# Gate and up in rows: block products for three of eight pairs of chunks, banks by role, weight buffers in halves

## The chip, the cores and the metric

One core of one Trainium2 chip runs the kernel. The time is device microseconds of one execution; it was measured three times, 2257.39 to 2257.93 us, median 2257.55 us. TensorE (PE) multiplies into eight banks of PSUM, VectorE (DVE) and ScalarE (ACT) work on SBUF and PSUM, GpSimd (POOL) does little here, and SyncE (SP) issues the loads.

## The reference

Two layers over 256 tokens of width 2048, all in float32. Each layer has a normed input projection (retention heads and a linear recurrence), an output projection added to x, and a gated feed-forward part of width 5632, which is 44 blocks of 128:

```
h = _rmsnorm(x, norm2_g[l])
x = x + (silu(h @ ffn_w_gate[l]) * (h @ ffn_w_up[l])) @ ffn_w_down[l]
```

A last norm follows. The change concerns `h @ w_gate` and `h @ w_up`, and how weights are prepared everywhere.

## The kernel before

Every weight matrix is read from memory once, in units of 1 MB (`Unit`): 128 columns of a matrix for all 16 chunks of 128 inputs, laid out as 128 x 2048. A unit is loaded into one of three raw buffers by SP (`load`, L551). `split` then makes two float32r tiles of it: ScalarE copies the upper part (`whi`, L568), VectorE subtracts it from the raw weight (`wlo`, L569), 1024 elements at a time. An activation is split in the same way into a pair (`pair`, L126 to L130). A product is then upper times upper, plus upper times lower, plus lower times upper.

In `column_unit` the weights are the loaded operand and the activations stream: L195 multiplies the upper weight chunk with both parts of the activation (512 columns), L198 the lower weight chunk with the upper activation (256 columns); two and two in turn, four such pairs to a block, 16 chunks to a unit. The result stands in a bank as columns of the layer (128 outputs by 256 tokens, twice) and is joined by `joined_halves` (L178, L179). `v_units` is the exception: there the activations are loaded (128 tokens) and 512 weight columns stream, three matmuls per chunk (L441 to L443), since v is wanted by rows.

The program of each engine is in order. `units` gives the order of the work: per layer v, the input projections, 16 units of the output projection, and then, three times (`THIRDS`), 15, 15 and 14 gate units in turn with as many up units, followed by 16 down units that use those 15 or 14 blocks. Ahead of block 0 and block 2 of a unit the loop issues the two splits of the unit two places later; `split` ends with the load of the unit three places after its own. Work that hangs on a result is put off by a number of blocks (`Ticks.after`). A gate unit ends in a scaling with the inverse root (L504) and a silu (L505); an up unit in two products (L509, L510) and the pair for the down projection.

The first of the output projection's units ends within the second one (`held`), because its last chunk comes late.

## Time and profile before

| | |
|---|---|
| median of three runs | 2257.55 us |
| the profiled execution | 2257.48 us, of it span 2255.7 us |
| PE busy | 2239.1 us, 99% |
| PE's weight loads | 1949.4 us, 86% |
| DVE busy | 1512.5 us, 67% |
| ACT busy | 1127.1 us, 50% |
| DMA | 187 GB/s over the span |
| granted TensorE clock | 0.998 of full speed |

Busy is the sum of an engine's instructions. Matmuls are pipelined, one begins before the one ahead of it is finished, so what a matmul costs is read from start to start in a timeline, not from its length. The same holds, by less, for VectorE and ScalarE.

### The profile page before, as it was taken

To read this page: it belongs to the slowest core of one execution; us is meant where nothing else is said; L and a number is where in the kernel's file an instruction comes from. 1 tells how busy PE (TensorE), PEld (TensorE's weight loads), DVE (VectorE), ACT (ScalarE), POOL (GpSimd) and SP (SyncE) were. 2 spreads that over 40 slices of the span, in tenths; PEclk is the share of its full clock that TensorE was granted. 3 is DMA by queue.
4 is the path that set the end of the run, shared out by engine and by line. 5 is a ranking of instruction groups with operands and counts; after the bars stand their busy time and mean duration, and the time that the engine had idled before them with its cause. 6 is when DMAs were issued, how large, how long until landed. Compare 5 with 4: busy or idle time off the path is not lost.

```text
span 2255.7 us, 31764 instructions
## 1 busy us (share of the span) xinstructions
PE 2239.1 (99%) x12760; PEld 1949.4 (86%) x12760; DVE 1512.5 (67%) x2405; ACT 1127.1 (50%) x1648; POOL 59.8 (3%) x97
## 2 busy tenths in 40 slices
PE   9999999999999999999999999999999999999997
PEld 7888888888888888888888888888888888888886
DVE  6888876666566655666748889766665666556665
ACT  6667544544344443444546665444443444334453
POOL 0010100000000000000000101000000000000000
PEclk9999999999999999999999999999999999999999
DMA  7555555555555555555555554555555555555553
GB/s 286 183 186 181 172 195 191 183 191 189 184 200 187 186 186 189 188 190 179 201 193 179 180 197 165 189 182 192 191 183 195 188 187 184 192 188 190 193 175 112
DMA packets 63140, 422.92 MB, mean 187 GB/s; under 512 B 7312, under 2 KB 7952, under 8 KB 24592
## 3 DMA queue, kind: packets, MB, share of 16 engines
q1 hardware_dynamic: 60912, 414.60, 52.5%
q0 software_dynamic: 1792, 5.24, 0.8%
q8 instruction: 100, 1.64, 0.3%
q10 hardware_dynamic: 288, 1.05, 0.1%
q14 instruction: 48, 0.39, 0.0%
HBM read 418.77 MB, written 2.10 MB: 187 GB/s over the span
## 4 chain that ended last, share of the span: by engine, by line
PE 97%; DVE 1%; issue 0%; DMA 0%; POOL 0%; ACT 0%; SPq 0%; DVEq 0%; POOLq 0%
PE acc_ps L195 62%; PE acc_ps L198 31%; PE v_ps L442 1%; PE v_ps L443 1%; PE v_ps L441 1%; PE sm_ps L331 1%; DVE wlo L569 0%; PE sm_ps L240 0%; DMA raw<-in_w_v_dram 0%; DVE op L130 0%; PE sm_ps L289 0%; PE sm_ps L157 0%; PE sm_ps L241 0%; PE sm_ps L256 0%; PE sm_ps L255 0%
## 5 line engine op out<-in xcount | busy, mean ns | idle before, releaser
L195 PE MATMUL acc_ps<-op,whi 128*128 128x512 f32 x6016 | 1899.8, 397 | 0.0
L198 PEld LDWEIGHTS acc_ps<-op,wlo 128*128 128x128 f32 x6016 | 1129.8, 188 | 263.4
L569 DVE TENSOR_TENSOR wlo<-raw,whi 128x1024 fp32r<-128x1024 f32 (+3 forms) x808 | 950.0, 1187 | 366.6 <-ACT whi L568 362.4
L198 PE MATMUL acc_ps<-op,wlo 128*128 128x256 f32 x6016 | 1188.6, 278 | 0.0
L568 ACT ACTIVATE whi<-raw 128x1024 fp32r<-128x1024 f32 (+3 forms) x808 | 817.3, 1029 | 657.3 <-PE acc_ps L195 578.1
L195 PEld LDWEIGHTS acc_ps<-op,whi 128*128 128x128 f32 x6016 | 920.4, 189 | 4.8 <-DVE op L127 0.7
L406 DVE TENSOR_TENSOR x<-acc_ps,x 128x256 f32<-128x256 f32 x128 | 54.2, 424 | 215.5 <-PE acc_ps L198 215.5
L126 ACT ACTIVATE op<-mix 128x256 fp32r<-128x256 f32 x104 | 43.1, 416 | 167.7 <-DVE mix L510 163.5
L505 ACT ACTIVATE sg<-z 128x256 f32<-128x256 f32 x88 | 36.8, 419 | 161.1 <-DVE z L504 161.1
L179 DVE TENSOR_TENSOR z<-acc_ps,low 128x256 f32<-128x256 f32 x256 | 106.7, 417 | 0.0
L178 ACT ACTIVATE low<-acc_ps 128x256 f32<-128x256 f32 x256 | 93.7, 366 | 0.0
L127 DVE TENSOR_TENSOR op<-mix,op 128x256 fp32r<-128x256 f32 x104 | 44.0, 424 | 42.7 <-ACT op L126 42.6
L509 DVE TENSOR_TENSOR sg<-sg,rs 128x256 f32<-128x256 f32 x88 | 37.4, 425 | 42.6 <-ACT sg L505 42.6
L407 DVE TENSOR_TENSOR x<-acc_ps,x 128x256 f32<-128x256 f32 x128 | 54.2, 424 | 4.3
L150 POOL TENSOR_TENSOR rc<-rc,mhalf 128x2 f32<-128x2 f32 x7 | 5.8, 824 | 1720.7 <-DVE rc L149 1720.7
L442 PE MATMUL v_ps<-wlo,op 128*128 128x512 f32 x128 | 50.1, 391 | 1.1 <-DVE wlo L569 1.1
L441 PE MATMUL v_ps<-whi,op 128*128 128x512 f32 x128 | 50.1, 396 | 0.5 <-ACT op L129 0.4
L443 PE MATMUL v_ps<-whi,op 128*128 128x512 f32 x128 | 50.1, 391 | 0.0
L510 DVE TENSOR_TENSOR mix<-z,sg 128x256 f32<-128x256 f32 x88 | 36.7, 417 | 0.0
L504 DVE TENSOR_TENSOR z<-z,rs 128x256 f32<-128x256 f32 x88 | 36.7, 417 | 0.0
L129 ACT ACTIVATE op<-x,par 128x256 fp32r<-128x256 f32 x64 | 31.2, 496 | 2.6 <-DMA par<-in_par_dram 1.8
L173 DVE TENSOR_TENSOR acc<-acc,sq 128x256 f32<-128x256 f32 x73 | 30.6, 420 | 1.6 <-ACT sq L172 1.0
(116 smaller groups left out, 698.9 us busy)
## 6 DMA issues: line engine op xcount, KB each, us to landing
raw<-in_w_gate_dram SPq DMA_DIRECT2D x88, 1024.0 KB, 4.8
raw<-in_w_up_dram SPq DMA_DIRECT2D x88, 1024.0 KB, 4.8
raw<-in_w_in_dram SPq DMA_DIRECT2D x80, 1024.0 KB, 4.8
raw<-in_w_down_dram SPq DMA_DIRECT2D x64, 960.0 KB, 4.7
raw<-in_w_out_dram SPq DMA_DIRECT2D x32, 1024.0 KB, 4.8
raw<-in_w_down_dram SPq DMA_DIRECT2D x32, 896.0 KB, 4.6
raw<-in_w_v_dram SPq DMA_DIRECT2D x12, 1024.0 KB, 4.8
raw<-in_w_v_dram SPq DMA_DIRECT2D x16, 256.0 KB, 6.0
```

Source lines behind the costliest of these rows:

```text
L127: V.tensor_tensor(out=t[:, 1, :], in0=x_ap, in1=t[:, 0, :].bitcast(F32), op=ALU.subtract)
L178: S.activation(out=low, in_=ps[:, T : 2 * T], func=AF.Copy)
L179: V.tensor_tensor(out=z, in0=ps[:, 0:T], in1=low, op=ALU.add)
L195: PE.matmul(u.ps, lhsT=u.hi[:, k * P : (k + 1) * P], rhs=operand(k).rearrange("p a t -> p (a t)"), start=k == order[0], stop=False)
L198: PE.matmul(u.ps[:, T : 2 * T], lhsT=u.lo[:, k * P : (k + 1) * P], rhs=operand(k)[:, 0, :], start=False, stop=k == order[-1])
L406: V.tensor_tensor(out=X[:, k, :], in0=ps[:, T : 2 * T], in1=X[:, k, :], op=ALU.add)
L407: V.tensor_tensor(out=X[:, k, :], in0=ps[:, 0:T], in1=X[:, k, :], op=ALU.add)
L441: PE.matmul(ps, lhsT=x2[:, 0, t], rhs=u.hi[:, w], start=k == 0, stop=False)
L442: PE.matmul(ps, lhsT=x2[:, 0, t], rhs=u.lo[:, w], start=False, stop=False)
L443: PE.matmul(ps, lhsT=x2[:, 1, t], rhs=u.hi[:, w], start=False, stop=k == KD - 1)
L568: S.activation(out=u.hi[:, w], in_=u.raw[:, w], func=AF.Copy)
L569: V.tensor_tensor(out=u.lo[:, w], in0=u.raw[:, w], in1=u.hi[:, w].bitcast(F32), op=ALU.subtract)
```

## The change

The feed-forward part is cut in 44 / 4 = 11 slabs per layer, four blocks of gate and the same four of up, 8 MB of weights (`slab_units`); the thirds become 16, 16 and 12 blocks. Within a slab a unit is no longer one block of outputs with 16 chunks, but one pair of chunks with four blocks of gate and four of up (512 columns each). The activations are the loaded operand, as for v. Gate and up of 256 tokens form a 2 x 2 arrangement of blocks: two halves of tokens, two chunks of inputs, on the other side gate and up. For pairs 0, 1 and 2 this is done with seven block products in place of eight: VectorE forms sums and differences of the raw weights (`up_parts`, `first_sums`), which are split like other weights, and four sums of blocks of the activations once per layer (`combined`). Pairs 3 to 7 are plain, eight products. The order of pairs is 0, 3, 1, 4, 2, 5, 6, 7.

The results of a slab fill all eight banks, each bank by its role; the next slab takes over banks in the order in which they come free (`start`, `columns_again`). `shared` forms the parts that several results have in common, `gate` and `up` end them, in rows, and TensorE transposes the product back to columns (`columns`), from which the pairs for the down projection are made (`operands_of`).

The weight tiles are six halves of 1024 instead of three of 2048, given back and taken half by half in one fixed order (`prepare`, at most two ahead of each block). The load of a pair of chunks consists of two DMAs in runs of 256 elements. `hold` puts the last blocks of the first units of the output and down projections behind the other blocks of their group.

The first excerpt is from PE's program, where the second pair of chunks, or the second slab, begins. Before, at the start of a gate unit (`acc_ps` is its bank, `op` the activations, `whi` and `wlo` the weights):

```order
L195 MATMUL acc_ps_4305<-op_3181,whi_4202 128x512
L195 MATMUL acc_ps_4305<-op_3205,whi_4202 128x512
L198 MATMUL acc_ps_4305<-op_3181,wlo_4203 128x256
L198 MATMUL acc_ps_4305<-op_3205,wlo_4203 128x256
L195 MATMUL acc_ps_4305<-op_3254,whi_4202 128x512
L195 MATMUL acc_ps_4305<-op_3303,whi_4202 128x512
```

Now, at the start of the second slab (`row_ps` are the banks, `s01` the sums of activations, `cb` and `ca` the finished rows of the slab before):

```order
L616 MATMUL row_ps_4360<-whi_4255,op_3260 128x512
L617 MATMUL row_ps_4360<-wlo_4256,op_3260 128x512
L618 MATMUL row_ps_4360<-whi_4255,op_3260 128x512
L616 MATMUL row_ps_4373<-whi_4271,s01_3305 128x512
L617 MATMUL row_ps_4373<-wlo_4272,s01_3305 128x512
L618 MATMUL row_ps_4373<-whi_4271,s01_3305 128x512
L731 MATMUL sm_ps_4364<-ident_82,cb_4242 128x128
L616 MATMUL row_ps_4377<-whi_4290,s01_3305 128x512
L617 MATMUL row_ps_4377<-wlo_4291,s01_3305 128x512
L731 MATMUL sm_ps_4364<-ident_82,ca_4241 128x128
L731 MATMUL sm_ps_4364<-ident_82,cb_4242 128x128
L731 MATMUL sm_ps_4364<-ident_82,ca_4241 128x128
```

The streaming operand is now always 512 weight columns, the bank changes every three matmuls (every six in a plain pair), and four transposes of the slab before stand among the products.

DVE's program, before, for an up unit and parts of its neighbours (two splits of 1024 per unit, the rest ends the results):

```order
L569 TENSOR_TENSOR wlo<-raw,whi 128x1024
L504 TENSOR_TENSOR z<-z,rs 128x256
L509 TENSOR_TENSOR sg<-sg,rs 128x256
L569 TENSOR_TENSOR wlo<-raw,whi 128x1024
L179 TENSOR_TENSOR z<-acc_ps,low 128x256
L569 TENSOR_TENSOR wlo<-raw,whi 128x1024
L510 TENSOR_TENSOR mix<-z,sg 128x256
L127 TENSOR_TENSOR op<-mix,op 128x256
```

Now, near the end of the first slab, where the next slab's fast pair is prepared (L206 are the splits, L649, L654 and L655 the differences of raw weights, L707 to L714 the ends of the slab):

```order
L708 TENSOR_TENSOR cb<-row_ps,cb 128x512
L206 TENSOR_TENSOR wlo<-raw,whi 128x1024
L709 TENSOR_TENSOR cb<-cb,ca 128x512
L649 TENSOR_TENSOR raw<-raw 128x8x128
L710 TENSOR_TENSOR ca<-ca,cb 128x512
L206 TENSOR_TENSOR wlo<-raw,whi 128x512
L654 TENSOR_TENSOR raw<-raw 128x4x128
L655 TENSOR_TENSOR raw<-raw 128x4x128
L206 TENSOR_TENSOR wlo<-raw,whi 128x1024 x2
L714 TENSOR_TENSOR ca<-row_ps,ca 128x512
L714 TENSOR_TENSOR cb<-row_ps,cb 128x512
L206 TENSOR_TENSOR wlo<-raw,whi 128x1024
```

The differences of a fast pair and the ends of the slab stand in one queue with the splits; a split that follows L655 has none of the others between.

The core of the diff:

```diff
-THIRDS = [(0, 15), (15, 15), (30, 14)]
+THIRDS = [(0, 16), (16, 16), (32, 12)]
+SLAB = 4
+FAST = 3
 RAW = 3
+HALVES = 6
...
-    hi_p = pool("whi", 3)
-    lo_p = pool("wlo", 3)
+    hi_p = pool("whi", HALVES)
+    lo_p = pool("wlo", HALVES)
...
+    def half_tiles(u, h):
+        u.hi[h] = hi_p.tile([P, 1024], F32R, tag="whi", name="whi")
+        u.lo[h] = lo_p.tile([P, 1024], F32R, tag="wlo", name="wlo")
+        return u.hi[h], u.lo[h]
+    def parts(hi, lo, raw):
+        S.activation(out=hi, in_=raw, func=AF.Copy)
+        V.tensor_tensor(out=lo, in0=raw, in1=hi.bitcast(F32), op=ALU.subtract)
+    def plain_halves(u, width):
+        def prep(h):
+            w = width // 2
+            hi, lo = half_tiles(u, h)
+            parts(hi[:, :w], lo[:, :w], u.raw[:, h * w : (h + 1) * w])
+        u.preps = [lambda: prep(0), lambda: prep(1)]
...
+    def hold(group):
+        rest = []
+        for u in group[:-1]:
+            fn, frees = u.blocks.pop()
+            then, u.done = u.done, None
+            def late(fn=fn, then=then):
+                fn()
+                then()
+            rest.append((late, frees))
+        tail = group[-1].blocks.pop()
+        group[-1].blocks += rest + [tail]
...
+    def combined(p, gains):
+        r = one_p.tile([P, 4, T], F32, tag="rot4", name="asum")
+        for i in range(2):
+            S.activation(out=r[:, i, :], in_=X[:, 2 * p + i, :], func=AF.Copy, scale=gains(2 * p + i))
+        a11, a21, a12, a22 = (r[:, i, j * P : (j + 1) * P] for i in range(2) for j in range(2))
+        f = r[:, 2:4, :].rearrange("p a (b t) -> p (a b) t", b=2)
+        V.tensor_tensor(out=f[:, 0, :], in0=a21, in1=a22, op=ALU.add)
+        V.tensor_tensor(out=f[:, 1, :], in0=f[:, 0, :], in1=a11, op=ALU.subtract)
+        V.tensor_tensor(out=f[:, 2, :], in0=a11, in1=a21, op=ALU.subtract)
+        V.tensor_tensor(out=f[:, 3, :], in0=a12, in1=f[:, 1, :], op=ALU.subtract)
+        if p == 0:
+            st["s01"] = one_p.tile([P, 2, 4, 2, P], F32R, tag="v", name="s01")
+        if p == 2:
+            st["s2"] = one_p.tile([P, 4, 2, P], F32R, tag="gy0", name="s2")
+        t = st["s2"] if p == 2 else st["s01"][:, p]
+        S.activation(out=t[:, :, 0, :], in_=f, func=AF.Copy)
+        V.tensor_tensor(out=t[:, :, 1, :], in0=f, in1=t[:, :, 0, :].bitcast(F32), op=ALU.subtract)
+        st["sums", p] = t
...
+            for f in range(f0, f0 + nf, SLAB):
+                res += slab_units(l, f, f == f0)
+            res[-1].done = columns_again
+            first = len(res)
...
+        def start():
+            if first:
+                free, later = list(turn["small"]), list(turn["big"])
+            else:
+                free, later = st["free"], st["later"]
+            ids = dict(zip((1, 2, 3, 8), free))
+            ids.update(zip((5, 4, 7, 6), later))
+            c["ids"] = ids
+            turn["small"] = [ids[8]]
+            st["free"] = [ids[i] for i in (1, 5, 7, 6)]
+            st["later"] = [ids[i] for i in (2, 4, 3, 8)]
+        def product(i, x, w, go, end):
+            if i not in c:
+                c[i] = bank(c["ids"][i], "row_ps")
+                go = True
+            ps = c[i]
+            PE.matmul(ps, lhsT=x[0], rhs=w[0], start=go, stop=False)
+            PE.matmul(ps, lhsT=x[0], rhs=w[1], start=False, stop=False)
+            PE.matmul(ps, lhsT=x[1], rhs=w[0], start=False, stop=end)
...
+        def loader(p):
+            def load(raw):
+                for i, name in enumerate(("w_gate", "w_up")):
+                    src = a[name][l, f0 : f0 + SLAB, :, 2 * p * P : (2 * p + 2) * P]
+                    nc.sync.dma_start(out=raw[:, i * 1024 : (i + 1) * 1024].rearrange("p (f w) -> p f w", f=SLAB),
+                                      in_=src.rearrange("f p w -> p f w"))
+            return load
...
+        turns = [q for p in range(FAST) for q in (p, FAST + p)] + list(range(2 * FAST, KD // 2))
+        for p in turns:
+            u = Unit(loader(p))
+            plain = p >= FAST
+            if not plain:
+                def gate_parts(u=u):
+                    hi, lo = half_tiles(u, 0)
+                    parts(hi, lo, u.raw[:, 0:1024])
+                def up_parts(u=u):
+                    hi, lo = half_tiles(u, 1)
+                    flat = lambda t: t[:, 0:512].rearrange("p (f w) -> p f w", f=SLAB)
+                    parts(flat(hi), flat(lo), piece(u.raw[:, 1024:2048], 1))
+                    r = u.raw.rearrange("p (c f k w) -> p c f k w", c=2, f=SLAB, k=2)
+                    V.tensor_tensor(out=r[:, :, :, 0, :], in0=r[:, 1].rearrange("p f k w -> p k f w"),
+                                    in1=r[:, :, :, 0, :], op=ALU.subtract)
+                def first_sums(u=u):
+                    g, p_ = u.raw[:, 0:1024], u.raw[:, 1024:2048]
+                    V.tensor_tensor(out=piece(p_, 1), in0=piece(p_, 1), in1=piece(g, 0), op=ALU.subtract)
+                    V.tensor_tensor(out=piece(g, 1), in0=piece(g, 1), in1=piece(p_, 1), op=ALU.subtract)
+                    hi, lo = half_tiles(u, 2)
+                    parts(hi, lo, g)
+                def second_sums(u=u):
+                    hi, lo = half_tiles(u, 3)
+                    parts(hi, lo, u.raw[:, 1024:2048])
+                u.preps = [gate_parts, up_parts, first_sums, second_sums]
+                def run(todo, p=p, u=u):
...
+                        w = {1: (0, 0), 2: (0, 1), 5: (2, 0), 4: (2, 1), 7: (3, 0), 6: (3, 1)}
+                        for i in todo:
+                            if i == 3:
+                                t = tuple(t[1][:, 0:512] for t in (u.hi, u.lo))
+                            else:
+                                h, k = w[i]
+                                t = piece(u.hi[h], k), piece(u.lo[h], k)
+                            product(i, x[i](), t, False, p == FAST - 1 and i in (1, 5, 6, 7))
+                    return go
+                for todo, frees in (((1, 2), [0]), ((3, 5), [1]), ((4, 7), [2]), ((6,), [3])):
+                    u.add(run(todo), frees)
+                if p == FAST - 1:
+                    u.done = lambda: tk.after(1, shared)
+            else:
+                plain_halves(u, 2048)
+                for j, side, i in ((0, 0, 2), (1, 0, 4), (0, 1, 3), (1, 1, 8)):
+                    def go(j=j, side=side, i=i, p=p, u=u):
+                        for k in range(2):
+                            product(i, block_of(j, 2 * p + k), (piece(u.hi[side], k), piece(u.lo[side], k)),
+                                    False, p == KD // 2 - 1 and k == 1)
+                        if p == KD // 2 - 1:
+                            tk.after(1, {2: lambda: gate(0), 4: lambda: gate(1), 3: lambda: up(0), 8: lambda: up(1)}[i])
+                    u.add(go, [side] if j else [])
+            res.append(u)
...
+        def shared():
+            c["a"] = one_p.tile([P, 2, 512], F32, tag="gy1", name="ca")
+            c["b"] = one_p.tile([P, 2, 512], F32, tag="rot4", name="cb")
+            m1, m5, u2, u3 = c["a"][:, 0, :], c["a"][:, 1, :], c["b"][:, 0, :], c["b"][:, 1, :]
+            S.activation(out=m1, in_=c[1], func=AF.Copy)
+            S.activation(out=m5, in_=c[5], func=AF.Copy)
+            V.tensor_tensor(out=u2, in0=c[6], in1=m1, op=ALU.add)
+            V.tensor_tensor(out=u3, in0=c[7], in1=u2, op=ALU.add)
+            V.tensor_tensor(out=u2, in0=u2, in1=m5, op=ALU.add)
+            V.tensor_tensor(out=m5, in0=m5, in1=u3, op=ALU.add)
+        def gate(j):
+            t, i = ((c["a"][:, 0, :], 2), (c["b"][:, 1, :], 4))[j]
+            V.tensor_tensor(out=t, in0=c[i], in1=t, op=ALU.add)
+            S.activation(out=t, in_=t, func=AF.Silu, scale=st["rsc"][:, j : j + 1])
+        def up(j):
+            g = (c["a"][:, 0, :], c["b"][:, 1, :])[j]
+            t, i = ((c["b"][:, 0, :], 3), (c["a"][:, 1, :], 8))[j]
+            V.tensor_tensor(out=t, in0=c[i], in1=t, op=ALU.add)
+            V.scalar_tensor_tensor(out=t, in0=t, scalar=st["rsc"][:, j : j + 1], in1=g, op0=ALU.mult, op1=ALU.mult)
+            c["act", j] = t
+            if j == 1:
+                tk.after(1, lambda: columns(0))
+        def columns(i):
+            ps = small()
+            for f in range(2):
+                for j in range(2):
+                    at = (2 * f + j) * P
+                    PE.transpose(ps[:, at : at + P], c["act", j][:, (2 * i + f) * P : (2 * i + f + 1) * P], ident)
+            tk.after(1, lambda: operands_of(i, ps))
+        def operands_of(i, ps):
+            for f in range(2):
+                st["act", f0 + 2 * i + f] = pair(ps[:, f * T : (f + 1) * T])
+            if i == 0:
+                tk.after(1, lambda: columns(1))
...
+    def prepare(most):
+        for _ in range(most):
+            i = at["next"]
+            if i >= len(items) or i - HALVES >= at["free"]:
+                return
+            n, u, h = items[i]
+            u.preps[h]()
+            if h == len(u.preps) - 1:
+                load(n + RAW)
+            at["next"] += 1
...
+                prepare(2)
             block()
+            for v, h in frees:
+                free[where[id(v), h]] = True
+            while at["free"] < len(items) and free[at["free"]]:
+                at["free"] += 1
```

## Rows read from the trace of the kernel before

**Rows 1.** The page, part 1: busy us (share of span) x instructions of each engine.

```profile
PE 2239.1 (99%) x12760; PEld 1949.4 (86%) x12760; DVE 1512.5 (67%) x2405; ACT 1127.1 (50%) x1648; POOL 59.8 (3%) x97
```

**Rows 2.** The page, part 4: the chain that ended last, by engine.

```profile
PE 97%; DVE 1%; issue 0%; DMA 0%; POOL 0%; ACT 0%; SPq 0%; DVEq 0%; POOLq 0%
```

**Rows 3.** Waits of PE: engine, line, releaser, us in total, times, longest; six kinds.

```profile
PE sm_ps L289 <- DVE on L275: 2.1, 2, 1.0
...
PE v_ps L441 <- ACT op L129: 0.4, 2, 0.2
```

**Rows 4.** Timeline: start us, us, engine, line, what; silu of two following gate units.

```profile
455.14 0.42 ACT L505 ACTIVATE sg<-z 128x256 f32<-128x256 f32 x1 [1.87 <-DVE z L504]
...
466.29 0.42 ACT L505 ACTIVATE sg<-z 128x256 f32<-128x256 f32 x1 [1.88 <-DVE z L504]
```

**Rows 5.** Windows: one gate and one up unit; PE, PEld, DVE, ACT, POOL busy.

```profile
408.50:419.65 11.15, 11.15 (x67) 9.73 (x66) 6.91 (x11) 5.40 (x9) 0.00 (x0) 1.00 0.53 187
```

**Rows 6.** Timeline of PE, a gate unit, two steps.

```profile
451.44 0.39 PE L198 MATMUL acc_ps<-op,wlo 128*128 128x256 f32 x2
...
452.13 0.40 PE L198 MATMUL acc_ps<-op,wlo 128*128 128x256 f32 x2
```

**Rows 7.** Timeline of PE, projection of v, nine matmuls, first and last.

```profile
1138.20 0.39 PE L442 MATMUL v_ps<-wlo,op 128*128 128x512 f32 x1
...
1140.02 0.39 PE L441 MATMUL v_ps<-whi,op 128*128 128x512 f32 x1
```

**Rows 8.** Timeline of PE around two transposes (line 289).

```profile
1421.90 0.40 PE L198 MATMUL acc_ps<-op,wlo 128*128 128x256 f32 x2
1422.14 0.38 PE L289 MATMUL sm_ps<-ident,on 128*128 128x128 f32 x2
1422.27 0.71 PE L195 MATMUL acc_ps<-op,whi 128*128 128x512 f32 x2
1422.82 0.40 PE L198 MATMUL acc_ps<-op,wlo 128*128 128x256 f32 x2
```

**Rows 9.** Timeline of DVE, a gate unit.

```profile
452.08 1.23 DVE L569 TENSOR_TENSOR wlo<-raw,whi 128x1024 fp32r<-128x1024 f32 x1 [1.64 <-ACT whi L568]
453.22 0.42 DVE L179 TENSOR_TENSOR z<-acc_ps,low 128x256 f32<-128x256 f32 x1
453.56 1.22 DVE L569 TENSOR_TENSOR wlo<-raw,whi 128x1024 fp32r<-128x1024 f32 x1
```

**Rows 10.** Timeline of DVE at the start: splits of 512.

```profile
14.57 0.48 DVE L130 SCALAR_TENSOR_TENSOR op<-x,par,op 128x256 fp32r<-128x256 f32 x1
14.96 0.68 DVE L569 TENSOR_TENSOR wlo<-raw,whi 128x512 fp32r<-128x512 f32 x1
15.56 0.48 DVE L130 SCALAR_TENSOR_TENSOR op<-x,par,op 128x256 fp32r<-128x256 f32 x1
```

**Rows 11.** Timeline of DVE: the second waits for the first.

```profile
562.43 0.42 DVE L406 TENSOR_TENSOR x<-acc_ps,x 128x256 f32<-128x256 f32 x1 [0.71 <-PE acc_ps L198]
562.89 0.42 DVE L407 TENSOR_TENSOR x<-acc_ps,x 128x256 f32<-128x256 f32 x1
```

**Rows 12.** Timeline of DVE at the end: four operations of 3 x 256.

```profile
2246.72 3.55 DVE L673 TENSOR_TENSOR x<-x,sm_ps 128x768 f32<-128x768 f32 x4 [1.99 <-ACT rs L670]
```

**Rows 13.** Timeline of ACT: the upper part that the split at 452.08 waits for.

```profile
450.99 1.06 ACT L568 ACTIVATE whi<-raw 128x1024 fp32r<-128x1024 f32 x1 [1.00 <-PE acc_ps L195]
451.95 0.36 ACT L178 ACTIVATE low<-acc_ps 128x256 f32<-128x256 f32 x1
```

**Rows 14.** Windows at the start; DMA share and GB/s stand last.

```profile
3.00:5.00 2.00, 2.00 (x11) 2.00 (x11) 0.64 (x1) 0.63 (x1) 0.00 (x0) 1.00 0.93 259
7.00:9.00 2.00, 1.75 (x7) 1.16 (x7) 1.54 (x7) 0.97 (x3) 0.00 (x0) 1.00 1.05 394
```

**Rows 15.** The page, part 6: loads of gate weights, KB each, us to landing.

```profile
raw<-in_w_gate_dram SPq DMA_DIRECT2D x88, 1024.0 KB, 4.8
```

**Rows 16.** Windows: the output projection of the first layer.

```profile
306.30:395.40 89.10, 89.10 (x517) 77.86 (x516) 63.03 (x98) 44.61 (x66) 0.69 (x1) 1.00 0.53 190
```

More of the change, by code (lines that the diff above doesn't have):

```diff
@@ L71, with __init__, add @@
 class Unit:
-    def __init__(self, src, width, blocks, done=None, begin=None):
-        self.src, self.width, self.blocks = src, width, blocks
-        self.done, self.begin = done, begin
-        self.split_at = (0, 2)
+    def __init__(self, load, begin=None, done=None, preps=()):
+        self.load, self.begin, self.done = load, begin, done
+        self.preps = list(preps)
+        self.blocks = []
+        self.hi, self.lo = {}, {}
+    def add(self, fn, frees=()):
+        self.blocks.append((fn, [(self, h) for h in frees]))
 @with_exitstack
@@ L99, in tmp, with bank, next_bank @@
         return (two_p if tag in TWO else one_p).tile([P, n], dtype, tag=tag, name=tag)
+    turn = {"big": [0, 1, 2, 3], "small": [4, 5, 6, 7]}
+    def bank(i, name):
+        return banks.tile([P, 512], F32, tag=f"b{i}", name=name)
+    def next_bank(kind):
+        i = turn[kind].pop(0)
+        turn[kind].append(i)
+        return bank(i, "acc_ps" if kind == "big" else "sm_ps")
     def small():
-        return sm_ps.tile([P, 512], F32, tag="sm", name="sm_ps")
+        return next_bank("small")
     par = const.tile([P, NPAR], F32, name="par")
@@ L180, in joined_halves @@
         return z
+    def half_tiles(u, h):
[11 more added lines that the diff above has]
+        u.preps = [lambda: prep(0), lambda: prep(1)]
     def column_unit(src, n_k, operand, done, begin=None, order=None):
-        u = Unit(src, n_k * P, [], begin=begin)
+        width = n_k * P
+        u = Unit(lambda raw, w=slice(0, width): nc.sync.dma_start(out=raw[:, w], in_=src[:, w]), begin=begin)
+        plain_halves(u, width)
         order = order or list(range(n_k))
+        side = lambda k: k // (n_k // 2)
+        col_of = lambda k: slice(k % (n_k // 2) * P, (k % (n_k // 2) + 1) * P)
+        last = {side(k): i // 4 for i, k in enumerate(order)}
         def block(i):
@@ L374, in y_done @@
             z = joined_halves(ps)
[L375 removed]
+            if n % 4 == 0:
+                st["y4"] = one_p.tile([P, 4, T], F32, tag=f"gy{n // 4}", name="y")
+            y = st["y4"][:, n % 4, :]
             st["y", l, n] = y
@@ L453, in evacuate @@
                         )
-                u.blocks = [block(kk) for kk in range(4)]
+                for kk in range(4):
+                    u.add(block(kk), [kk // 2] if kk % 2 else [])
                 if s == 3:
@@ L525, in last_sums, with columns_again @@
+    def columns_again():
+        free, later = st["free"], st["later"]
+        turn["big"] = free[:3] + later[:1]
+        turn["small"] = free[3:] + later[1:]
     def last_sums():
@@ L547, in load @@
             u.raw = raw_p.tile([P, 2048], F32, tag="raw", name="raw")
-            pieces = 4 if n < 4 else 1
-            for q in range(pieces):
-                w = slice(q * u.width // pieces, (q + 1) * u.width // pieces)
-                nc.sync.dma_start(out=u.raw[:, w], in_=u.src[:, w])
-                if n == 0:
-                    nc.sync.dma_start(out=X[:, q, :], in_=a["x"][:, q])
-                    if q == 0:
-                        nc.sync.dma_start(out=par, in_=a["par"])
+            if n < 4:
+                for q in range(4):
+                    u.load(u.raw, slice(q * 512, (q + 1) * 512))
+                    if n == 0:
+                        nc.sync.dma_start(out=X[:, q, :], in_=a["x"][:, q])
+                        if q == 0:
+                            nc.sync.dma_start(out=par, in_=a["par"])
+            else:
+                u.load(u.raw)
             if n < 3:
@@ L621, in operands @@
     def operands(n, q):
-        split(n, q, 4)
+        quarter(n, q)
         k = 4 * n + q
@@ L646, in trunk @@
         tk.after(30 + i, part)
+    items = [(n, u, h) for n, u in enumerate(units) for h in range(len(u.preps))]
+    where = {(id(u), h): i for i, (n, u, h) in enumerate(items)}
+    free = [False] * len(items)
+    at = {"next": 8, "free": 0}
+    def prepare(most):
[8 more added lines that the diff above has]
+            at["next"] += 1
     for n, u in enumerate(units):
@@ L650, in trunk @@
             u.begin()
-        for b, block in enumerate(u.blocks):
+        for b, (block, frees) in enumerate(u.blocks):
             if n < 3:
```

109 lines of the change are left out of this document (50 added, 59 removed).

## The prediction

> **What bounds the kernel now.** I read the shares of the engines first, then the chain that ended last, then who TensorE waits for, and only then the timelines that give a price for one instruction. TensorE is busy for 99% of the span [rows 1] and carries 97% of the chain [rows 2]; all its waits for other engines together come to about 7 us, the longest kind 2.1 us [rows 3]. So a column taken from TensorE is time gained, and VectorE (67%) is the next engine to look at.
>
> The stage that changes is gate and up. One gate unit and one up unit follow each other every 466.29 - 455.14 = 11.15 us [rows 4], so eight units (four gate, four up: what the change calls a slab of four) take 44.6 us, and the 22 slabs of both layers 981 us. In this stage VectorE is busy 6.91 of 11.15 us, 62% [rows 5].
>
> **TensorE in the new form.** Before, four matmuls (two of 512 columns, two of 256) start 452.13 - 451.44 = 0.69 to 0.70 us apart [rows 6]; a unit has eight such steps, 5.57 us. The new form works in rows: the activations are the loaded operand and 512 weight columns stream. The projection of v already does that, and its matmuls start (1140.02 - 1138.20) / 8 = 0.2275 us apart [rows 7]. I count 0.227. A fast pair of chunks has 7 products of 3 matmuls, a plain one 8 products of 3: 3 x 21 + 5 x 24 = 183 matmuls per slab against 192 without the block products, hence 41.5 us. In rows the result has to be turned back: 8 transposes per slab. Two of them stretch one step from 0.70 to 1422.82 - 1421.90 = 0.92 us [rows 8], so 0.1 us each, 0.8 us per slab. TensorE's price is 42.3 us per slab, 2.3 us less than now; 22 slabs, -51 us. That is the gain if nothing else is late.
>
> The rows of v read their streaming operand in one piece; the new products read four pieces of 128 columns. No row shows that. From below it costs nothing (512 columns are 512 columns); from above each piece behaves like a matmul of its own: two transposes of 128 start 0.13 us apart as a pair [rows 8], 0.065 us each, 4 x 0.065 = 0.26 us per product matmul, +6.0 us per slab. I take nothing, the end that the rows of v are nearest to (same shape, same 512 columns; for VectorE too a second dimension in an access has no price, below), and keep +6.0 as a rival.
>
> **VectorE in the new form.** This is where the change is paid. Its prices, start to start: a split of 1024 elements 453.22 - 452.08 = 1.14 us [rows 9]; one of 512 0.60 us and a scalar_tensor_tensor of 256 with a scalar from a column 0.39 to 0.40 us, against 0.34 for a plain 256 [rows 9, 10]; an operation that waits for the one just before it pays about 0.12 more (0.46 for 256) [rows 11]. Four operations of 3 x 256 take 3.55 us together [rows 12], 0.89 us each; the line through 1.14 and 0.60 (0.06 us plus 1.05 ns per element) gives 0.87 for 768 elements: a second dimension in the access costs nothing.
>
> Per slab: 19 splits of 1024 (three in each fast pair, two in each plain one), 21.7 us; 3 splits of 512, 1.8; 3 differences of 1024 (line 649 of the new kernel), 3.4; 6 of 512 that wait for each other (654, 655), 6 x 0.72 = 4.3; the four shared sums, 2.5; four sums that end gate and up, 2.4; two products with the inverse root, 1.3; four lower parts of the operands, 1.4. That is 38.8 us. On top comes one stall in each fast pair: the split of the first sums needs ScalarE's upper part, and ScalarE can't begin it before VectorE's last difference is done; nothing stands between in VectorE's queue. ScalarE's 1024 start 1.09 us ahead of the split that waits for it [rows 9, 13], with the handover 1.2 us, three times 3.6 us. VectorE's price is 42.4 us per slab, where today it is 62% of 44.6, 28 us [rows 5].
>
> So the two engines come out within 0.1 us of each other, and that is the core of the forecast: neither waits for the other for long only if they stay in step. Six half buffers let VectorE run ahead by six halves, and a half is prepared as one is given back. In the first five units of a slab VectorE is slower than TensorE (3 x 7.8 + 2 x 2.3 us of weights plus about 3 us left from the slab before, 31, against 3 x 21 + 2 x 24 matmuls, 25.2), in the last three faster (6.8 plus 5 of the ends, against 16.3); a lead of six halves (7.8 + 2.3 = 10.1 us) covers the 6 us. The sum over a slab therefore decides, not its worst part, and every third starts with a full lead from the down projection, where VectorE has little to do. I take 42.7 us per slab: 42.3 for the six slabs that start a third and about 42.9 for the other sixteen, where small misfits between two full queues show. 22 x (44.6 - 42.7) = 42 us less. Bounds for this term: 42.3 (TensorE alone) below; above, every VectorE operation that isn't priced with its wait already (39 of 45) paying its whole duration (1.22 instead of 1.14 [rows 9]), +3.1 us, 45.5.
>
> The Trainium skill has a rule that speaks against this (VectorE: DVE Perf Modes, section "The DRAIN you can't avoid"): after an operation the next one does not start until the pipe is empty. By it VectorE would take that upper bound, 22 x (45.5 - 44.6) = 20 us slower than today. The trace disagrees: the next operation starts 1.14 us after one that lasts 1.22 or 1.23, 0.08 us before its end, as the page itself allows for operations that are not held.
>
> **ScalarE and the loads.** ScalarE's 19 upper parts of 1024 are 0.96 us each [rows 13], with the rest some 25 us per slab: hidden under 42 us. A load becomes two of 512 KB in runs of 1 KB instead of one of 1 MB in runs of 8 KB. Where the trace loads runs of 1 to 4 KB, at the start, it moved 259 GB/s in the worst two microseconds and 394 in the best [rows 14]: 4.0 to 2.7 us per MB, under the 5.3 us of a unit. Landing is 4.8 us now [rows 15]; a stream slower by up to 4.0 - 2.7 = 1.3 us and a second issue make up to 6.5. The tightest place is the load for the next slab's first pair, issued when the third last unit is split: four splits and the four shared sums later it is needed, 7.0 us. I count nothing.
>
> The Trainium skill (Perfetto Trace Analysis, section "DMA Optimizations") warns that transfers under 2 KB carry a significant overhead each. The start of this trace agrees in direction (259 against 394 GB/s), not far enough to pass 5.3 us.
>
> **The rest.** The sums of blocks of h2 (three times per layer, in the output projection) add 4 small operations, one split of 512 and one wait for ScalarE: about 3 us of VectorE each, 9 per layer, beside 89.1 - 63.0 = 26 us that VectorE is idle there [rows 16]. No rows of h2's inverse root are spread any more: 4 short matmuls less per layer, under 1 us. Thirds of 16, 16 and 12 stream the same 44 chunks; the last slab's operands come in four steps, one per block of four chunks, 4 x 1.4 = 5.6 us after its last product, and the down blocks that need them are held back behind six others, 8.4 us. Nothing counted.
>
> The profiled execution has a span of 2255.7 us in a time of 2257.48, which is the median of the three runs (2257.55) within 0.1. Forecast: 2257.5 - 42 = 2215 us.
>
> **Rivals.**
> 1. TensorE alone decides. VectorE's lead covers all, and the slab falls to 42.3 us: 2257.5 - 51 = 2206. For it: the sums are equal and the down projection refills the lead. Against it: VectorE has no slack left in the middle slabs. Chance 0.20.
> 2. VectorE decides, and loses. Its queue is in order, and in the steady slab it holds splits that wait for ScalarE, which waits for TensorE to give back the half six places earlier; behind a late split stand the operations that end gate and up, the transposes wait for these, and TensorE stands behind the transposes. The change loses from 44.6 us per slab, 2.2 us or 5% over the sum; at the upper bound of 45.5 it is 22 x 0.9 = 20 us slower, 2277. For it: no slack, 45 operations; against it: the prices are of a full queue already [rows 9]. Chance 0.11.
> 3. The loads decide: at over 5.4 us per MB (under 195 GB/s) TensorE waits; at half of the 394 GB/s, 5.3 us, it is even, and at 6 us a slab takes 48 and the kernel 2257.5 + 75 = 2332. Against it: the worst window has 259. Chance 0.03.
> 4. The pieces of 128 in the streaming operand cost TensorE 6.0 us per slab: 48.3, +81 us, 2339. Chance 0.03.
> 5. The gain is just eaten (a slab of 44.4 to 44.8): 2253 to 2262. Chance 0.04.
>
> **How the numbers follow.** The forecast's chance is 0.59, its own range 2206 to 2240 (42.3 to 43.8 us per slab). 0.2% is what a measurement of this kernel can tell from no change, 4.5 us. Faster: 0.59 + 0.20 + 0.02 of the second rival that ends between 43.8 and 44.4 = 0.81; the same 0.04; slower 0.15. The range for 8 in 10 reaches from 2200 (42.0 us per slab, some of the transposes' price hidden) to 2250 (44.2 us per slab, VectorE 4% over its sum).
>
> **What would show it.** Gate and up windows with TensorE at 42.3 to 43.3 us per slab and VectorE at over 90% busy there; row matmuls 0.227 us apart; a split of 1024 at 1.14; VectorE idle before the first-sums split by about 1.1 us, 66 times. TensorE's waits, where there are any, should name VectorE (line 206 or 721), not a load. It is wrong if the row matmuls are over 0.235 us apart, if the strided differences (649, 654, 655) take over 5% more than their elements, or if VectorE waits for loads.

## The result, and the profile after

The changed kernel takes 2218.71 us (median of four, 2218.25 to 2219.35) against 2257.74 us beside it: a ratio of 0.983, 95% interval 0.981 to 0.984. That is 39 us less; the two profiled spans, 2255.7 and 2217.2 us, differ by 38.5. The forecast was 2215.

The page of the changed kernel, its parts on busy time and on the chain of waits by engine; they answer to [rows 1, 2]:

```profile
PE 2195.4 (99%) x11322; PEld 1861.6 (84%) x11322; DVE 1774.3 (80%) x2545; ACT 1214.4 (55%) x1620; POOL 47.5 (2%) x97
```

```profile
PE 81%; DVE 10%; issue 4%; ACT 2%; DMA 2%; POOL 0%; SPq 0%; ACTq 0%; DVEq 0%; POOLq 0%
```

TensorE is still busy for 99%, but VectorE has risen from 67 to 80% of the span, and the chain, which ran 97% over TensorE, now runs 10% over VectorE. The gain shows slab by slab. The windows of four slabs (from a slab's first row product to the next one's; the columns are length, busy time and count by engine, granted clock, DMA share, GB/s):

```profile
core 0: us, PE busy (x) PEld busy (x) DVE busy (x) ACT busy (x) POOL busy (x), PEclk, DMA share, GB/s
650.50:692.00 41.50, 41.50 (x185) 34.34 (x184) 36.10 (x39) 23.24 (x26) 0.00 (x0) 1.00 0.62 200
692.00:734.70 42.70, 42.70 (x193) 34.96 (x193) 38.41 (x46) 24.43 (x31) 0.00 (x0) 1.00 0.59 192
734.70:777.60 42.90, 42.79 (x192) 34.93 (x191) 38.73 (x46) 24.53 (x31) 0.00 (x0) 1.00 0.61 197
1831.10:1874.80 43.70, 42.83 (x193) 34.92 (x192) 39.22 (x46) 25.13 (x32) 0.00 (x0) 1.00 0.61 195
```

A slab was 44.6 us [rows 4]. The windows are cut some 0.2 us ahead of the row products. Read from the starts of the row products themselves, a slab that starts a third takes 41.6 us (42.1 at the start of a layer), the others 42.5 to 43.7; in the later ones shown VectorE is busy for 90%. The 22 slabs come to 937.4 us, 42.61 each. In the kernel before, gate and up read in the same way, from their first product to the first one of the down projection, are 982.7 us in six stretches, of which this is the first:

```profile
388.80:556.90 168.10, 168.10 (x971) 146.75 (x970) 103.93 (x152) 82.25 (x123) 0.69 (x1) 1.00 0.53 186
```

So the slabs give 45.3 us. Outside them 6.9 us are given back: 2.5 ahead of the output projections, 4.4 in the down projections.

TensorE's timeline inside a slab, three row products in a row:

```profile
700.83 0.39 PE L616 MATMUL row_ps<-whi,op 128*128 128x512 f32 x1
701.05 0.39 PE L617 MATMUL row_ps<-wlo,op 128*128 128x512 f32 x1
701.28 0.39 PE L618 MATMUL row_ps<-whi,op 128*128 128x512 f32 x1
```

Over the slabs the median from start to start is 0.227 us, as for v [rows 7], although the streaming operand now consists of four pieces. Whom TensorE, its weight loads (PEld) and ScalarE wait for (total, times, longest):

```profile
PE sm_ps L731 <- DVE cb L721: 2.8, 5, 0.9
...
PEld sm_ps L731 <- DVE cb L721: 8.2, 15, 1.3
...
ACT whi L205 <- DVE raw L655: 232.0, 66, 4.8
```

TensorE's largest kind of wait is a transpose that waits for VectorE's last product of gate and up. The third row is ScalarE's side of the stall that the prediction places in each fast pair: 66 times ScalarE waits for VectorE's last difference. One of them, in VectorE's timeline and, the last row, ScalarE's:

```profile
770.59 0.69 DVE L654 TENSOR_TENSOR raw<-raw 128x512 f32<-128x512 f32 x1
771.31 0.69 DVE L655 TENSOR_TENSOR raw<-raw 128x512 f32<-128x512 f32 x1
773.21 2.36 DVE L206 TENSOR_TENSOR wlo<-raw,whi 128x1024 fp32r<-128x1024 f32 x2 [1.21 <-ACT whi L205]
...
772.12 2.01 ACT L205 ACTIVATE whi<-raw 128x1024 fp32r<-128x1024 f32 x2 [4.25 <-DVE raw L655]
```

ScalarE has waited 4.25 us for the second difference, and VectorE then waits 1.21 us for ScalarE. In VectorE's whole timeline this wait is 1.2 us long at 60 of the 66 fast pairs.

### The profile page after: what moved, and what is told of

It is laid out like the page before. It is cut to its first block, busy times and chain, and to the rows that moved or that the text cites. A ratio compares the mean times of both kernels' runs of the same rounds, so it can differ in the third digit from the quotient of the medians.

```text
span 2217.2 us, 29753 instructions
## 1 busy us (share of the span) xinstructions
PE 2195.4 (99%) x11322; PEld 1861.6 (84%) x11322; DVE 1774.3 (80%) x2545; ACT 1214.4 (55%) x1620; POOL 47.5 (2%) x97
## 4 chain that ended last, share of the span: by engine, by line
PE 81%; DVE 10%; issue 4%; ACT 2%; DMA 2%; POOL 0%; SPq 0%; ACTq 0%; DVEq 0%; POOLq 0%
PE acc_ps L233 32%; PE acc_ps L236 16%; PE row_ps L618 9%; PE row_ps L616 9%; PE row_ps L617 9%; DVE wlo L206 5%; ACT whi L205 2%; DMA raw<-in_w_gate_dram 2%; PE acc_ps L524 1%; PE acc_ps L525 1%; PE acc_ps L523 1%; PE sm_ps L731 1%; DVE raw L649 1%; DVE raw L654 1%; DVE raw L655 1%
## 5 line engine op out<-in xcount | busy, mean ns | idle before, releaser
L205 ACT ACTIVATE whi<-raw 128x1024 fp32r<-128x1024 f32 (+2 forms) x940 | 918.4, 1005 | 842.8 <-PE acc_ps L233 439.6
L206 DVE TENSOR_TENSOR wlo<-raw,whi 128x1024 fp32r<-128x1024 f32 (+2 forms) x940 | 1064.9, 1157 | 290.9 <-ACT whi L205 285.0
L233 PE MATMUL acc_ps<-op,whi 128*128 128x512 f32 x3200 | 1014.1, 398 | 0.0
L236 PEld LDWEIGHTS acc_ps<-op,wlo 128*128 128x128 f32 x3200 | 600.7, 188 | 140.8
L236 PE MATMUL acc_ps<-op,wlo 128*128 128x256 f32 x3200 | 630.2, 278 | 0.0
L233 PEld LDWEIGHTS acc_ps<-op,whi 128*128 128x128 f32 x3200 | 490.1, 189 | 1.6
L617 PE MATMUL row_ps<-wlo,op 128*128 128x512 f32 x1078 | 420.9, 390 | 0.0
L616 PE MATMUL row_ps<-whi,op 128*128 128x512 f32 x1078 | 420.1, 390 | 0.0
L618 PE MATMUL row_ps<-whi,op 128*128 128x512 f32 x1078 | 419.9, 390 | 0.0
L616 PEld LDWEIGHTS row_ps<-whi,op 128*128 128x128 f32 x1078 | 202.3, 188 | 42.2
L618 PEld LDWEIGHTS row_ps<-whi,op 128*128 128x128 f32 x1078 | 202.4, 188 | 41.9
L617 PEld LDWEIGHTS row_ps<-wlo,op 128*128 128x128 f32 x1078 | 202.4, 188 | 41.6
L618 PE MATMUL row_ps<-whi,s 128*128 128x512 f32 x264 | 104.8, 397 | 0.0
L616 PE MATMUL row_ps<-whi,s 128*128 128x512 f32 x264 | 103.4, 392 | 0.0
L649 DVE TENSOR_TENSOR raw<-raw 128x1024 f32<-128x1024 f32 x66 | 80.6, 1221 | 0.1
```

What stands on the lines that cost most here:

```text
L205: S.activation(out=hi, in_=raw, func=AF.Copy)
L206: V.tensor_tensor(out=lo, in0=raw, in1=hi.bitcast(F32), op=ALU.subtract)
L233: PE.matmul(u.ps, lhsT=u.hi[side(k)][:, col_of(k)], rhs=operand(k).rearrange("p a t -> p (a t)"), start=k == order[0], stop=False)
L236: PE.matmul(u.ps[:, T : 2 * T], lhsT=u.lo[side(k)][:, col_of(k)], rhs=operand(k)[:, 0, :], start=False, stop=k == order[-1])
L616: PE.matmul(ps, lhsT=x[0], rhs=w[0], start=go, stop=False)
L617: PE.matmul(ps, lhsT=x[0], rhs=w[1], start=False, stop=False)
```

## The experiments

Theory: TensorE sets the length of a slab (183 matmuls at 0.227 us and the transposes), and VectorE, nearly as long, adds little waits on top. Rivals: the form or the buffers bring the gain, VectorE sets the length, or the loads do.

**e1: columns again, the rest of the change kept.** `slab_units` is replaced by the gate and up units of before, and the block sums of the activations go.

```
-            for f in range(f0, f0 + nf, SLAB):
-                res += slab_units(l, f, f == f0)
-            res[-1].done = columns_again
+            for f in range(f0, f0 + nf):
+                ... gate unit, up unit as before
```

> Gate and up go back to columns by plain products (192 of 512 columns for each slab, one 128-column matmul block at a time), while the halves, the hold, the thirds and the banks of the changed kernel stay. Theory T (the whole gain is the form of the gate and up products): the slab is back at 44.6 us, so the gain goes: 2257 us, within 3. Rival R (the buffers in halves and the order of loads and thirds bring part of the gain by themselves): 2225 to 2250 us.

Measured: 2258.47 us, ratio to before 1.0001 (0.9992 to 1.0011). Halves, holds and thirds are worth nothing by themselves, as theory T has it. Two small terms cancel in that: the input projections take 1.9 us longer than before (490.9 for 489.0), the down projections 1.3 us less (548.9 for 550.2).

**e2: rows without block products** (`FAST = 0`; gate and up end straight from PSUM).

```
-FAST = 3
+FAST = 0
-            V.tensor_tensor(out=t, in0=c[i], in1=t, op=ALU.add)
-            S.activation(out=t, in_=t, func=AF.Silu, ...)
+            S.activation(out=t, in_=c[i], func=AF.Silu, ...)
```

> Rows with no block products at all: 192 matmuls of 512 columns for each slab. Theory T: 192 x 0.227 = 43.6 us and 1.0 us of transposes and small waits make 44.6 us for each slab, as before; the transposes of the last slab of each layer fall into the next stage: 2255 us, between 2250 and 2262. Rival R (the row form itself is quicker than the column form, since one streaming operand serves a whole row): 42 us or less for each slab, under 2225 us. Rival V (VectorE set the length of the changed kernel's slabs): the sums' VectorE work goes with the block products, and the time is no longer than the changed kernel's, 2219 us or less.

Measured: 2259.30 us, 1.0005 (0.9995 to 1.0014). The slabs are 44.45 us in the mean, 977.8 in all, 4.9 us less than before by the same reading, and the time outside them takes that back. So the row form alone brings nothing: a slab without transposes in it (the first of a third) takes 43.5 us, and the transposes cost the other slabs 1.2 us each. The down projections take 554.4 us here, 5.5 more than in e1, so that part of the time outside the slabs belongs to the rows, not to the block products.

**e3: two fast pairs** (`FAST = 2`).

> Two of eight pairs of chunks by seven block products instead of three: 186 matmuls for each slab instead of 183, and one pair's sums less on VectorE. Theory T (TensorE sets the slab): 3 x 0.227 = 0.68 us more for each of 22 slabs, 15 us: 2234 us, between 2230 and 2237. Rival V (VectorE sets it): 5 us less of its work for each slab: 2219 us or less. Mixed (half the slab's small waits are VectorE's and go too): 2225 to 2230 us.

Measured: 2226.99 us, 0.9861 (0.9845 to 0.9878): the mixed case. Its windows, first and second slab of a third:

```profile
652.30:694.50 42.20, 42.20 (x188) 34.95 (x187) 32.03 (x35) 21.75 (x24) 0.00 (x0) 1.00 0.61 196
694.50:737.70 43.20, 43.20 (x195) 35.51 (x194) 34.92 (x41) 23.32 (x29) 0.00 (x0) 1.00 0.60 195
```

Here TensorE is not idle in these slabs: 186 x 0.227 = 42.2 us, and 1.0 for the transposes that follow from the slab before. The first two pairs bring 32 us against e2, where six matmuls of 0.227 us less in each of 22 slabs make 30; the third brings 8.3 of its 15. Of the 6.7 us that are missing, 2.0 are not VectorE's: the matmuls of the third fast pair are slower by 0.09 us per slab (last section). Some 4 us are, as e5 shows: its order takes 4.2 us from the slabs.

**e4: four fast pairs** (`FAST = 4`, the sums of the fourth in four small tiles).

> Four of eight pairs by seven block products: 180 matmuls for each slab, and one pair's sums more on VectorE. TensorE's work is 22 x 0.68 = 15 us less: 2204 us if TensorE still set the length. VectorE's windows of the changed kernel show 38.4 of 42.7 us busy; a pair's sums add about 5.5 us, so 43.9 us of work with no stall for a slab of 41.9. Theory T (VectorE takes over as soon as its work is more than TensorE's, with its stalls on top): 44.5 to 48 us for each slab, 2260 to 2335 us. Rival R (the stalls shrink when VectorE is late, since ScalarE runs ahead): 43.9 us for each slab, about 2245 us. Rival T2 (TensorE goes on setting it): 2204 us.

Measured: 2279.38 us, 1.0091 (1.0069 to 1.0112): theory T, VectorE with its stalls takes over. The windows of one slab, and of two stretches of 4 us within it:

```profile
746.70:795.30 48.60, 45.73 (x190) 35.04 (x189) 42.82 (x51) 25.25 (x32) 0.00 (x0) 0.96 0.53 174
...
750.70:754.70 4.00, 2.87 (x8) 1.58 (x8) 4.00 (x6) 4.00 (x6) 0.00 (x0) 0.90 0.46 157
754.70:758.70 4.00, 4.00 (x14) 3.02 (x13) 4.00 (x5) 0.02 (x1) 0.00 (x0) 0.67 0.31 106
```

TensorE is idle for 2.9 us of the slab, while VectorE has 42.8 us of work and stalls besides. 15 us less for TensorE became 61 us more than the changed kernel. Some of it is the granted clock, which fell in this slab and in two others of the profiled run: they took 48.2 to 48.6 us where the others like them took 47.0, 4 us in all.

**e5 and e11: the differences earlier.** `up_parts` computes the two further differences too, and the next plain pair's halves are split before those of the sums. The loads are still issued in the order of the units, so that the plain pair's waits for the fast pair's.

```
 up_parts:    V.tensor_tensor(out=r[:, :, :, 0, :], ...)
+             V.tensor_tensor(out=piece(p_, 1), ...)
+             V.tensor_tensor(out=piece(g, 1), ...)
 first_sums:
-             V.tensor_tensor(out=piece(p_, 1), ...)
-             V.tensor_tensor(out=piece(g, 1), ...)
 prepare, for a fast pair n:
-             halves (n,0) (n,1) (n,2) (n,3) (n+1,0) (n+1,1)
+             halves (n,0) (n,1) (n+1,0) (n+1,1) (n,2) (n,3)
```

> Each fast pair's two further differences (128 x 512 each, VectorE) are computed in the first half of its preparation, and the next plain pair's two halves come before the two halves of the sums, so that ScalarE no longer has to wait for the differences in the row of VectorE's work. The work stays the same. Theory V (what the changed kernel's slabs cost over 183 x 0.227 + 1.0 = 42.5 us is VectorE waiting for ScalarE after the differences): the some 7 us that its 22 slabs have above that go: 2212 us, between 2210 and 2215. Rival R (the wait only moves to the next place in the row, since VectorE's pure work is near the slab's length): 2217 to 2222 us.

Measured: 2214.61 us, 0.9808 (0.9793 to 0.9822): theory V. To have the small difference on one chip, both were run again:

> The changed kernel as it is, beside e11 on the same chip: 2218.7 us, within 1.

> The kernel of e5 again, beside e10: 2214.6 us, within 1, 3 to 5 us under e10. If the 4 us between e5 and the changed kernel came from another chip or hour, there is less than 2 us between them.

Measured: 2219.93 us (2219.41 to 2221.08) and 2214.14 us (2213.80 to 2214.44), 5.8 us apart and without overlap, a little more than was expected (the first of them came out 1.2 us higher than at its first timing). This is the fastest version. From the trace of e5, the windows of the slabs two and three of a third, the chain by engine, and ScalarE's waits for the differences:

```profile
691.70:734.30 42.60, 42.60 (x192) 34.88 (x191) 38.61 (x46) 24.75 (x31) 0.00 (x0) 1.00 0.61 198
734.30:777.00 42.70, 42.70 (x192) 34.92 (x192) 38.70 (x46) 24.84 (x31) 0.00 (x0) 1.00 0.61 198
```

```profile
PE 95%; issue 2%; DVE 1%; ACT 1%; POOL 0%; DMA 0%; SPq 0%; DVEq 0%; POOLq 0%
```

```profile
ACT whi L206 <- DVE raw L654: 93.8, 44, 3.7
```

VectorE's work is the same 38.6 us, but its share of the chain falls from 10 to 1%, and the slabs from 937.4 to 933.2 us. TensorE has no gap left in any of the 22; in the changed kernel the gaps come to 3.1 us.

**e6: one more VectorE difference per slab.**

```
 second_sums:  parts(hi, lo, u.raw[:, 1024:2048])
+              if p == FAST - 1: V.tensor_tensor(out=lo, ...)   # once more
```

> One more VectorE difference of 1024 columns for each slab, a repeat of the low part of the third pair's second sums: 22 x 1.14 us more VectorE work in all, and nothing else. Theory V (VectorE with its stalls is as long as TensorE in the slabs after the first of a third): the whole 1.14 us shows in the last two slabs of each third and part of it in the second: 12 to 18 us, 2231 to 2237 us. Rival R (the tenth of the window in which VectorE is idle takes it): 0 to 3 us, 2219 to 2222 us.

Measured: 2245.23 us, 0.9944 (0.9927 to 0.9961), about 26 us more than the changed kernel, where theory V expected 12 to 18. One part of the difference is the granted clock, which fell in two slabs of the profiled run. The windows of the second slab of the first and of the second third:

```profile
431.80:478.30 46.50, 44.66 (x192) 36.02 (x192) 39.40 (x47) 24.85 (x32) 0.00 (x0) 0.96 0.57 182
697.90:742.40 44.50, 43.04 (x192) 34.92 (x192) 40.66 (x48) 25.02 (x32) 0.00 (x0) 1.00 0.59 190
```

The slab with the fall is 2.0 us longer. The sixteen later slabs come to 710.2 us against 686.9; without the 4 us of the two falls that is 19 us, 1.2 us each, so the whole dose shows there, while the slabs that start a third stay at 41.6 to 42.1 us. ScalarE's waits for gate's loads, first in the changed kernel, then here (total, times, longest), have grown too:

```profile
ACT whi L205 <- DMA raw<-in_w_gate_dram: 10.8, 21, 1.8
```

```profile
ACT whi L206 <- DMA raw<-in_w_gate_dram: 90.1, 37, 5.1
```

A load is issued when the last half of a unit is split; a late VectorE asks late, and then waits for what it asked. How much of the 19 us goes by way of these waits isn't shown.

**e7: one load of 1 MB instead of two of 512 KB.**

```
-                for i, name in enumerate(("w_gate", "w_up")): ... two DMAs, runs of 1 KB
+                nc.sync.dma_start(out=raw, in_=a["w_gu"][l, f0 // SLAB, p])
```

> Gate's and up's chunks for a pair come in one load of 1 MB with 8 KB for each partition, from an array that is laid out for it, instead of two loads of 512 KB in pieces of 1 KB. Theory N (the loads are in time either way): 2218.7 us, within 1.5. Rival L (the rows of 1 KB make the loads late, which the 24 us of ScalarE's waits for them would be a sign of): 2205 to 2215 us.

Measured: 2219.47 us, 0.9831 (0.9816 to 0.9846): no difference. Runs of 1 KB are in time.

**e8 and e9: four fast pairs in e5's order, with and without GpSimd.** e8 puts the difference of 128 x 1024 on GpSimd and has e7's loads; e9 has neither.

```
-    V.tensor_tensor(out=r[:, :, :, 0, :], in0=r[:, 1]..., op=ALU.subtract)
+    G.tensor_tensor(out=r[:, :, :, 0, :], in0=r[:, 1]..., op=ALU.subtract)   # e8 only
```

> Four pairs by seven block products (180 matmuls for each slab), the order of e5 with the first difference of each fast pair (128 x 1024) on GpSimd instead of VectorE, and the whole loads of e7. TensorE: 180 x 0.227 + 1.0 = 41.9 us for each slab. VectorE: 38.4 + 5.5 - 4 x 1.22 = 39.0 us without stalls. Theory T (with VectorE's work under TensorE's and its stalls gone TensorE sets the slab): 15 us less than e5's theory V: 2197 us, between 2194 and 2205. Rival V (stalls remain, or GpSimd's difference, by the 725 ns of 128 x 256 some 2.9 us, comes late or slows VectorE): 43 to 45 us for each slab, 2225 to 2265 us.

> Four pairs by seven block products in the order of e5, all differences on VectorE, gate's and up's loads apart as in the changed kernel: e8 without GpSimd's part and without the whole loads. Theory V (in e4 the length came from VectorE's stalls on top of its work; in this order only its work of about 43.9 us for a slab is left, and in e8 it was GpSimd's part that stretched VectorE's own work): 41 us for a slab that starts a third, 43.9 to 45 for the others: 2228 to 2250 us. Rival R (e8 was slow for the order or the number of fast pairs, not for GpSimd): 2270 us or more.

Measured: e8 2325.86 us, 1.0300 (1.0285 to 1.0315), far worse than either theory; e9 2240.23 us, 0.9921 (0.9904 to 0.9937), in the range of theory V. The window of e9's third slab of a third:

```profile
738.90:783.80 44.90, 43.28 (x189) 34.18 (x189) 42.05 (x51) 25.80 (x32) 0.00 (x0) 1.00 0.58 188
```

So the order is worth 39 us at four fast pairs (e4 to e9; 33 between the profiled runs, of which 4 are e4's clock), and GpSimd's help costs 86, if e8's whole loads make as little difference here as in e7, at three fast pairs. VectorE's splits by form, first e8 then e9 (busy, mean ns):

```profile
L207 DVE TENSOR_TENSOR wlo<-raw,whi 128x1024 fp32r<-128x1024 f32 x816 | 1051.4, 1306 | 216.7 <-ACT whi L206 209.2 <-PE sm_ps L386 3.0
L207 DVE TENSOR_TENSOR wlo<-raw,whi 128x512 fp32r<-128x512 f32 x104 | 105.1, 1012 | 7.1 <-ACT whi L206 6.9
```

```profile
L207 DVE TENSOR_TENSOR wlo<-raw,whi 128x1024 fp32r<-128x1024 f32 x816 | 980.6, 1219 | 223.9 <-ACT whi L206 219.1 <-PE sm_ps L386 3.0
L207 DVE TENSOR_TENSOR wlo<-raw,whi 128x512 fp32r<-128x512 f32 x104 | 70.8, 683 | 4.8 <-ACT whi L206 4.8
```

The same instructions cost VectorE 105 us more, nearly as much as the 88 differences that GpSimd took over cost it in e9 (107.1 us). So VectorE isn't relieved: it is busy for 1868.6 us, in e9 for 1850.4. Two places in e8's timeline, GpSimd's row above VectorE's, show how:

```profile
674.15 2.73 POOL L654 TENSOR_TENSOR raw<-raw 128x1024 f32<-128x1024 f32 x1 [13.27 <-DVE wlo L207]
674.78 3.19 DVE L207 TENSOR_TENSOR wlo<-raw,whi 128x1024 fp32r<-128x1024 f32 x1 [0.16 <-ACT whi L206]
...
723.15 4.09 POOL L654 TENSOR_TENSOR raw<-raw 128x1024 f32<-128x1024 f32 x1 [13.18 <-ACT whi L206]
723.17 1.82 DVE L207 TENSOR_TENSOR wlo<-raw,whi 128x512 fp32r<-128x512 f32 x2
```

A split of 1.22 us that starts 0.63 us after GpSimd's difference lasts 3.19 us, and ends 1.09 us after GpSimd's end, so it can have done little until then. In the second place VectorE runs a split of 512 and one of 1024 at its usual pace (0.60 and 1.22 us), and GpSimd's operation lasts 1.4 us longer than in the first. The Trainium skill (SBUF — State Buffer, section "SBUF: two separate sides") states that the two engines share a pair of ports and that whichever of the two begins holds it for its whole instruction, where VectorE reads two inputs from SBUF. The first place agrees with that; in the second the two begin within 0.02 us of each other, too near to tell which was first. On top of this VectorE waits for GpSimd's result, 68.7 us over 32 waits.

## Why the prediction was right

- **TensorE's price.** 42.3 us per slab was forecast, 41.5 of it for the matmuls. In slabs without transposes these take 41.6, and the row pitch of 0.227 us is met. The transposes were put at 0.8 us per slab; they are 1.0 to 1.1 us, and fall into the next slab, or, behind the last slab of a third, among the down products. In e5, where TensorE has no gap in any slab, the slabs come to 933.2 us, and with 5.6 us of transposes in the down projections to 42.7 us each: 0.4 more than forecast.
- **Four pieces in the streaming operand.** Taken at nothing, and they cost nothing (0.227 us), so rival 4 falls.
- **VectorE's price.** 38.8 us without the stalls, against 38.4 to 39.2 busy in the windows of the later slabs. The strided differences cost what their elements cost, which the lines of the changed kernel show (busy, mean ns):

```profile
L649 DVE TENSOR_TENSOR raw<-raw 128x1024 f32<-128x1024 f32 x66 | 80.6, 1221 | 0.1
L655 DVE TENSOR_TENSOR raw<-raw 128x512 f32<-128x512 f32 x66 | 45.5, 690 | 1.7
L654 DVE TENSOR_TENSOR raw<-raw 128x512 f32<-128x512 f32 x66 | 45.5, 689 | 1.6
```

- **The stall and the two full queues.** A stall of 1.2 us was forecast, and it is there at 60 of the 66 fast pairs. The sixteen later slabs are 42.9 us each, as forecast, but the transposes in them cost more, and the waits less, than was thought. The six first are 250.5 / 6 = 41.7 instead of 42.3, since their transposes fall later. e3, e5 and e6 show how closely the two queues fit: with one fast pair fewer VectorE costs nothing, in an order without this stall it costs nothing, and 1.14 us more shows in full in the later slabs. Rival 1 (TensorE alone, 2206) would have needed e5's order, and even that ends at 2214.6, mainly because TensorE's own price was 0.4 us per slab too low. Rival 2 (VectorE decides and loses) is what happens at one fast pair more, in e4.
- **The loads.** e7 shows that they are in time; rival 3 falls. They come 3.6 and 5.1 us after their issue, against 4.8 for 1 MB [rows 15]. That the 259 GB/s at the start came from short runs, as the prediction reads it, no run shows; runs of 8 KB changed nothing in e7. The loads of the changed kernel:

```profile
raw<-in_w_gate_dram SPq DMA_DIRECT2D x176, 512.0 KB, 3.6
raw<-in_w_up_dram SPq DMA_DIRECT2D x176, 512.0 KB, 5.1
```

- **What was mis-sized, and some luck.** The gain of the spans is 38.5 us and not 22 x 1.9 = 42. A part is the transposes of the last slabs. e1 has the same thirds, halves and holds without rows; the down projections of the second third, first in e1, then in the changed kernel:

```profile
836.50:925.70 89.20, 89.20 (x514) 77.83 (x513) 52.48 (x65) 34.58 (x35) 0.00 (x0) 1.00 0.53 189
...
820.70:910.80 90.10, 90.10 (x522) 78.63 (x521) 56.84 (x73) 34.88 (x37) 0.00 (x0) 1.00 0.52 177
```

  The eight matmuls more are the transposes, and cost 0.9 us; over the six thirds the down projections are 554.5 us against 548.9. Counted with them, TensorE's price was 8.2 us too low over the 22 slabs, 2.0 of it for slower matmuls of the third fast pair (last section). Against that, 0.4 us per slab was allowed for misfits of the two queues, 8.8 us, and the changed kernel's slabs are only 4.3 us above e5's; and gate and up took 1.5 us more before than 22 x 44.6. "Nothing counted" for the rest was 1.2 us too little: the input projections take 1.9 us longer and begin 0.6 us later, the new thirds give 1.3 back. The 1.9 are in e1 too, so they don't come with the rows; what causes them was not taken apart. The sum, 8.2 - 4.5 - 1.5 + 1.2 = 3.4 us, is the miss. The mechanism was right, but that the forecast came this near is in part luck, since its errors cancel.

## What to carry to other kernels

Where an edit takes work from the busiest engine and gives some to the next, price both per stage, stalls included: here the two came out within 0.1 us of each other in the forecast, the third fast pair brought 8 us of its 15, and a fourth cost 61 where TensorE saved 15. At that point the order of the second engine's queue counts beside its amount: 22 operations more cost 26 us in e6, and moving two differences ahead of independent work gave 4 to 6 us at three fast pairs and 39 us at four (a part of it clock), with no instruction less. Before a helper engine takes over work, look at what it shares with the engine it is to relieve.

## What was not expected of the hardware

- GpSimd and VectorE held each other up to the full length of an operation (3.19 us for a split of 1.22 us), so that 88 differences on GpSimd, 2.8 us each, made the kernel 86 us slower.
- In e4 the granted clock fell: in a stretch in which TensorE was busy 2.87 of 4 us with 8 matmuls it was 0.90 of full speed, and in the next 4 us 0.67 in the mean, so in part the lower of the two levels, 1.2 GHz for 2.4, although TensorE was busy throughout. That slab took 48.6 us where most of the later slabs of its kernel took 47.0. The same happened in two slabs of e6, at 2.0 us each. In all slabs of the changed kernel and of e5 the clock stayed at 1.00. So waits that VectorE puts into TensorE's queue can cost more than their own length.
- The matmuls of the third fast pair are slower than the others. From its first matmul to the one 21 later, the second fast pair, then the third, in a slab of the changed kernel:

```profile
660.91 0.39 PE L616 MATMUL row_ps<-whi,op 128*128 128x512 f32 x1
...
665.67 0.39 PE L616 MATMUL row_ps<-whi,op 128*128 128x512 f32 x1
...
671.79 0.39 PE L616 MATMUL row_ps<-whi,op 128*128 128x512 f32 x1
...
676.64 0.39 PE L616 MATMUL row_ps<-whi,op 128*128 128x512 f32 x1
```

  That is 0.227 us each and then 0.231, 0.09 us more for the pair, in all 22 slabs and in e5 and e7 as well; TensorE has no gap there. In e3, with two fast pairs, both run at 0.227. Why is open.
